# Value products with stationary values, normalised probabilities, and expert weights through other pools

## The chip, the cores and the metric

One core of a Trainium2 chip runs the whole kernel. The metric is the device time of one execution in microseconds; the number of a kernel is the median of its runs. The engines named here are PE (TensorE, with its weight loads as PEld), DVE (VectorE), ACT (ScalarE), POOL (GpSimd) and SP (SyncE, which issues the DMAs).

## The reference

256 tokens of width 1024 pass two blocks of two layers each, all in float32. Cut to what matters here:

```python
# first block, layer i
q, k, v = project_qkv(x, w_qkv[i], cos, sin)            # 16 query heads, 4 key/value heads, 64 wide
a = moba_attention(q, k, v) if i == 0 else sliding_window_attention(q, k, v, sinks)
x = layer_norm(alpha * x + a @ w_o[i], ...)
f = swiglu(x, ...) if i == 0 else moe_swiglu(x, ...)    # 8 experts, top 2, d_ff 3584
x = layer_norm(alpha * x + f, ...)
x = x + (p[i] @ w_ple_proj[i]) * sigmoid(x @ w_ple_gate[i])
# sliding window
probs = e / (jnp.sum(e, axis=-1, keepdims=True) + jnp.exp(sink - m))
out = einsum('bnkgqj,bnjkd->bnqkgd', probs, vv)
# second block, layer l: gated delta rule and a dilated causal attention (8 heads, 64 wide), side by side,
# then a gated FFN with a short convolution
```

All three attentions are a softmax over scores and a product with the values. The mixture of experts reads all eight experts' weights, 8 x 3 x 1024 x 3584 numbers.

## The kernel before

The program is one long list of operations. A planner (class `Plan`) takes them with their data dependencies, gives every tile a slot of a pool and writes out an order for each engine; SP's DMAs are in one such order too. All operations are issued in one helper, so they all carry line 756 in the profile (ACT's copies line 754, the loads of expert counts line 751). The pools in SBUF that matter: `raw` (5 slots, weights as they come), `hi` and `lo` (the split of a weight into two rounded parts, 6 and 5), `v4`, `w4`, `kv` (4, 8 and 2 slots), and `mx` (15 slots), which takes the place of `hi`, `lo` and `r4` while the experts run. PSUM has pools A, B and C with 2, 4 and 2 banks.

**Attention of the first block** (`first_layer`, `att_pair`, `att_out`, `part_T`; layers 0 and 1). The 256 queries are two blocks b of 128, the 16 heads two parts of eight, each part two groups of four. For a block and a part, `att_pair` makes the scores of both groups side by side in PSUM (C and B), the negative maximum on DVE and exp on ACT. `att_out` then takes one group at a time: it transposes the probabilities P (PE, copies out of PSUM), multiplies the transposed probabilities, stationary with 128 queries, by the values of a head with a column of ones behind them (65 columns, `va`), once per head and key block (nk = b + 1 blocks), takes the reciprocal of the 65th column and multiplies the 64 others by it. That gives heads along the columns; `part_T` transposes the result again, four transposes per block and part, and splits it for w_o. w_o comes in chunks of 256 rows, 128 partitions each (`load`).

**Dilated attention** (`att_pair("dilated", ...)` in the second block's layers). The same for eight heads, once per layer and block, with pool A.

**Experts** (`moe`). `route` gives each token a position in its experts, the counts are loaded into PE registers (line 751) and the largest count decides a branch (`overflow_experts`, lines 1634 and 294), which isn't taken here. `gather_pair` makes one-hot matrices on DVE and gathers the tokens of two experts with matmuls. Then each expert takes its three matrices in 84 chunks of 128 rows, 512 KB each: gate and up in three passes of 1024 and one of 512 columns, and down between them. Up to 64 tokens of an expert run as 64 stationary columns against 512 weight columns, two column tiles side by side; if it has more, a conditional part (line 733) adds 32-column tiles. Experts 1, 3, 6 and 7 (counted from 0) take that part here; the others don't. The chunks land in a ring of slots: `raw_moe` is a string of 28 of them, in which m, r, w, v and k stand for `mx`, `raw`, `w4`, `v4` and `kv`. A slot is fetched into when its last user is done, and SP takes its fetches in order, so that one that waits holds up all behind it. Ahead of the experts `fetch` asks for the first 22 chunks, in `raw`, `kv` and `mx`.

## Time and profile before

| | us |
|---|---|
| median of 3 runs | 2221.87 (2221.15 to 2225.56) |
| the profiled execution | 2224.77 |
| its span | 2223.0 |
| PE busy | 2102.1 (95%) |
| DVE busy | 984.3 (44%) |
| ACT busy | 751.7 (34%) |
| POOL busy | 224.7 (10%) |
| DMA, mean over the span | 251 GB/s |

The terms of a sum are taken from the profiled execution and set against its 2224.77 us. Where its stages lie: layer 0's attention to about 110 us, its FFN to 400, layer 1's attention to 477, router and branch to 510, the experts to 1420, then the second block with its dilated attentions around 1600 to 1652 and 1975 to 2030. A busy PE is not a PE at its peak, and the DMA share is that of the packets' time over 16 engines: at 1.03 and some 408 GB/s the queues are full.

### The profile page before, as it was taken

What the parts mean: (1) busy time and instruction counts of PE and PEld (TensorE: products, weight loads), DVE (VectorE), ACT (ScalarE), POOL (GpSimd) and SP (SyncE); (2) the same over time, 40 slices, a digit from 0 to 9 for tenths busy, and PEclk for the clock granted to TensorE, in tenths of its full rate; (3) what the DMA queues carried; (4) which work ended last, traced back from release to release, by engine and by line L of the source; (5) the groups of instructions that cost most, each with busy time, mean ns of one, the idle gap of its engine ahead of it and who ended that gap; (6) DMA issues with size and microseconds to landing.
All of it is one profiled execution on the core that took longest, in us unless ns stands there. A gap on an engine that the chain in (4) does not pass through costs nothing. (4 is left out here: it accounts for less than half of the span.)

```text
span 2223.0 us, 35510 instructions
## 1 busy us (share of the span) xinstructions
PE 2102.1 (95%) x14582; PEld 1449.2 (65%) x14582; DVE 984.3 (44%) x1670; ACT 751.7 (34%) x1141; POOL 224.7 (10%) x147
## 2 busy tenths in 40 slices
PE   8999999988799989998979999899999999999998
PEld 6899997763334323433233434479979997988997
DVE  6665467651010101010101001467687768768666
ACT  5544444420011101110110000356465556456554
POOL 0110001120000000000000000218020005411000
PEclk9999999989899999999999999999999999999999
DMA  7356664349999999999999998544455664435563
GB/s 251 111 165 192 184 184 152 114 159 345 404 388 370 373 404 409 385 372 404 408 404 394 369 396 326 188 145 144 130 170 183 190 183 141 124 97 187 175 194 117
DMA packets 246476, 557.48 MB, mean 251 GB/s; under 512 B 21320, under 2 KB 108552, under 8 KB 246280
## 3 DMA queue, kind: packets, MB, share of 16 engines
q1 hardware_dynamic: 246280, 554.72, 69.9%
q8 instruction: 141, 2.31, 0.4%
q14 instruction: 55, 0.45, 0.1%
HBM read 553.60 MB, written 1.05 MB: 250 GB/s over the span
## 5 line engine op out<-in xcount | busy, mean ns | idle before, releaser
L756 DVE TENSOR_TENSOR lo<-raw,hi 128x1024 fp32r<-128x1024 f32 x324 | 404.7, 1257 | 200.3 <-PE B L756 94.6
L756 ACT ACTIVATE hi<-raw 128x1024 fp32r<-128x1024 f32 x364 | 382.2, 1062 | 292.8 <-PE B L756 123.5
L756 PE MATMUL B<-r,hi 128*128 128x256 f32 x2112 | 388.2, 282 | 0.0
L756 PEld LDWEIGHTS B<-r,hi 128*128 128x128 f32 x2112 | 342.0, 191 | 17.7
L756 PE MATMUL B<-mx,w 128*64 128x512 f32 (+3 forms) x2188 | 327.9, 458 | 10.6 <-DMA mx<-in_w_exp_up_dram 8.4
L756 PE MATMUL A<-hi,r 128*128 128x512 f32 x896 | 334.3, 410 | 0.9 <-DVE v L756 0.6
L756 PE MATMUL B<-r,lo 128*128 128x256 f32 x1056 | 298.6, 283 | 0.0
L756 PEld LDWEIGHTS B<-mx,w 128*32 128x32 f32 (+1 forms) x2188 | 111.0, 124 | 153.1 <-issue 104.3
L756 PEld LDWEIGHTS B<-r,lo 128*128 128x128 f32 x1056 | 201.5, 191 | 0.0
L756 PEld LDWEIGHTS A<-hi,r 128*128 128x128 f32 x896 | 171.1, 191 | 32.2 <-DVE v L756 1.4
L756 PE MATMUL C<-hi,r 128*128 128x512 f32 x512 | 185.1, 400 | 1.1 <-ACT kv L756 1.1
L756 DVE MEMSET B<- 128x256 f32 (+1 forms) x64 | 15.7, 245 | 370.0 <-ACT w L756 366.6
L756 PE MATMUL A<-lo,r 128*128 128x512 f32 x448 | 177.4, 396 | 0.2 <-DVE lo L756 0.2
L756 PE MATMUL B<-w,w 128*128 128x128 f32 (+4 forms) x1252 | 168.4, 363 | 0.3 <-PEq L733 0.3
L756 PE MATMUL A<-mx,v 128*32 128x256 f32 (+1 forms) x960 | 162.1, 491 | 0.2 <-PEq L733 0.2
L754 ACT ACTIVATE v<-C 128x512 f32<-128x512 f32 (+2 forms) x63 | 29.4, 467 | 379.8 <-PE C L756 336.0
L756 DVE TENSOR_TENSOR w<-w,B 128x256 f32<-128x256 f32 (+2 forms) x79 | 41.8, 529 | 247.9 <-PE B L756 229.7
L756 POOL TENSOR_TENSOR lo<-raw,hi 128x1024 fp32r<-128x1024 f32 x40 | 102.0, 2563 | 487.8 <-ACT hi L756 367.4
L756 PEld LDWEIGHTS B<-w,w 128*128 128x128 f32 (+2 forms) x1252 | 104.5, 155 | 51.4 <-issue 39.6
L756 ACT ACTIVATE w<-B 128x256 f32<-128x256 f32 (+3 forms) x95 | 44.7, 475 | 264.8 <-PE B L756 242.9
L756 PEld LDWEIGHTS C<-hi,r 128*128 128x128 f32 x512 | 98.5, 192 | 18.8 <-ACT kv L756 1.9
L756 PE MATMUL B<-raw,w 128*64 128x512 f32 (+3 forms) x648 | 100.9, 463 | 1.3 <-DMA raw<-in_w_exp_up_dram 1.0
(239 smaller groups left out, 2602.1 us busy)
## 6 DMA issues: line engine op xcount, KB each, us to landing
mx<-in_w_exp_up_dram SPq DMA_DIRECT2D x124, 512.0 KB, 10.2
mx<-in_w_exp_down_dram SPq DMA_DIRECT2D x120, 512.0 KB, 10.3
mx<-in_w_exp_gate_dram SPq DMA_DIRECT2D x119, 512.0 KB, 8.0
raw<-in_ffn_up_dram SPq DMA_DIRECT2D x88, 512.0 KB, 3.7
raw<-in_w_in_dram SPq DMA_DIRECT2D x56, 512.0 KB, 3.8
raw<-in_w_exp_down_dram SPq DMA_DIRECT2D x48, 512.0 KB, 10.2
w<-in_w_exp_up_dram SPq DMA_DIRECT2D x46, 512.0 KB, 10.2
raw<-in_ffn_down_dram SPq DMA_DIRECT2D x44, 512.0 KB, 4.5
```

The costliest lines, as they stand in the source:

```text
L754: eng.activation(args[0], args[1], AF.Copy)
L756: getattr(eng, method)(*args, **kw)
```

## The change

- In all attentions the values are the stationary operand now, in 64 columns, without the column of ones. The transposed probabilities of a group stream past: four heads at once (512 columns) in the first block, where the four share a key/value head, one head (128 columns) in the dilated attention. The two groups write the two halves of one PSUM tile (`att_values`), heads along the partitions, so the second transposition is gone and `split_ps` reads the result.
- Since a row of the result no longer belongs to one query, the probabilities are normalised ahead: exp adds up its row (`accum_out`), DVE takes the reciprocal and multiplies P, 128x512 at a time. The sink's share is added before that.
- The rows of w_o come in the heads' new order: two transfers over 64 partitions for each chunk (`by_heads`).
- Expert weights: the ring is 24 slots of `mx`, `raw` and `w4`; `v4` and `kv` are no longer in it. Ahead of the experts 28 chunks are asked for, 7 of them (into `raw` and `kv`) before the switch of the region.
- The count loads have no bounds check, and the first one-hot matrices are made before the branch.

The diff, cut to that:

```diff
         if method == "values_load":
-            kw["to"].cell[0] = self.nc.values_load(args[0], engines=[mybir.EngineType.PE], min_val=0, max_val=S)
+            kw["to"].cell[0] = self.nc.values_load(args[0], engines=[mybir.EngineType.PE],
+                                                       skip_runtime_bounds_check_because="it is the sum of 256 zeros and ones")
...
-        self.raw_first = [("raw", RAW)] * RAW + [("kv", 2)] * 2 + [("mx", 15)] * 15
-        size = {"m": ("mx", 15), "r": ("raw", RAW), "w": ("w4", 8), "v": ("v4", 4), "k": ("kv", 2)}
-        self.raw_moe = [size[c] for c in "mrmwmrmvmwmkmrmwmrmvmwmkmrmm"]
+        self.raw_first = [("raw", RAW)] * RAW + [("kv", 2)] * 2 + [("mx", 15)] * 15 + [("w4", 8)] * 4 + [("v4", 4)] * 2
+        size = {"m": ("mx", 15), "r": ("raw", RAW), "w": ("w4", 8)}
+        self.raw_moe = [size[c] for c in "mrmwmmrmwmmrmwmmrmwmmrmm"]
         self.fetched = {}
-        self.ahead = []
+        self.ahead, self.by_heads = [], False
...
             r0 = k0 + 128 * m * h
-            nc.sync.dma_start(raw, lambda r0=r0: w[span(r0, 128 * m), span(c0, n)].rearrange("(t p) c -> p t c", p=128))
+            if self.by_heads:
+
+                for s in range(2):
+                    r0 = k0 + 256 * s + 64 * m * h
+                    nc.sync.dma_start(raw[64 * s:64 * s + 64], w[r0:r0 + 64 * m, c0:c0 + n].rearrange("(t p) c -> p t c", p=64))
+            else:
+                nc.sync.dma_start(raw, lambda r0=r0: w[span(r0, 128 * m), span(c0, n)].rearrange("(t p) c -> p t c", p=128))
             raws.append(raw)
...
-        va = self.nc.tile([128, 2, HK, 65], F32, "va", "kv", 2)
-        self.nc.gpsimd.memset(va, 1.0)
+        va = self.nc.tile([128, 2, HK, 64], F32, "va", "kv", 2)
         return qT, kT, va
...
+                hs = slice(i0, i0 + per)
+                for i in range(i0, i0 + per):
+                    nc.scalar.activation(P[:, i], ps[:, i - i0], AF.Exp, bias=nm[:, i:i + 1], accum_out=den[:, i])
+                if kind == "swa":
+                    es = self.sm([128, per, 1], "es")
+                    nc.vector.tensor_tensor(out=es[:, :, 0], in0=ns, in1=self.nsink[:, 4 * g + i0:4 * g + i0 + per], op=OP.subtract)
+                    nc.scalar.activation(es, es, AF.Exp)
+                    nc.vector.tensor_tensor(out=den[:, hs], in0=den[:, hs], in1=es, op=OP.add)
+                nc.vector.reciprocal(den[:, hs], den[:, hs])
+                part = P[:, hs].rearrange("p i k j -> p i (k j)")
+                nc.vector.tensor_tensor(out=part, in0=part, in1=den[:, hs].to_broadcast([128, per, nk * 128]), op=OP.mult)
+        self.att_values(kind, va, b, [(heads, P) for _, heads, P, _, _ in groups], [t[k] for t in aT.tiles])
...
-        po = (self.pb if grouped else self.pa)([128, 4, 65], "po")
-        for i in range(4):
-            for kb in range(nk):
-                nc.tensor.matmul(po[:, i, :], lhsT=PT[:, i, kb, :], rhs=va[:, kb, heads[i][3], :],
-                                 start=kb == 0, stop=kb == nk - 1)
...
-        nc.vector.tensor_tensor(out=o, in0=po[:, :, 0:64], in1=den.to_broadcast([128, 4, 64]), op=OP.mult)
...
+        pool = self.pb if grouped else self.pa
+        PT = [self.heads_last(P, nk, pool) for _, P in groups]
+        po = pool([128, 4, 128], "po")
+        with nc.group():
+            for i in range(1 if grouped else 4):
+                hs = slice(None) if grouped else i
+                for kb in range(nk):
+                    for s, (heads, _) in enumerate(groups):
+                        nc.tensor.matmul(po[64 * s:64 * s + 64, hs], lhsT=va[:, kb, heads[i][3], :], rhs=PT[s][:, hs, kb, :],
+                                         start=kb == 0, stop=kb == nk - 1)
+        self.split_ps(po, *[t[:, :, b * 128:b * 128 + 128] for t in dst])
...
-    def gather_pair(self, e, xs, pos):
-
-        nc = self.nc
+    def pair_one_hots(self, e, pos):
+
         P = self.r2([128, 2, 256], "P")
         for j in range(2):
             for b in range(2):
-                nc.vector.tensor_scalar(P[:, b, 128 * j:128 * j + 128], self.iota, pos[:, b, e + j:e + j + 1], None, op0=OP.is_equal)
+                self.nc.vector.tensor_scalar(P[:, b, 128 * j:128 * j + 128], self.iota, pos[:, b, e + j:e + j + 1], None, op0=OP.is_equal)
+        return P
+
...
         self.raw_tags = self.raw_first
-        for name, c0, n in (("gate", 0, 8), ("up", 0, 8), ("gate", 1024, 6)):
-            for k in range(n):
-                key = "w_exp_" + name, 0, 128 * k, c0
-                self.raws = len(self.fetched) - 1
-                self.fetched[key] = self.weights(*key[:3], 1, c0, 1024)
+        keys = [("w_exp_" + name, 0, 128 * k, c0) for c0 in (0, 1024) for name in ("gate", "up") for k in range(KT)]
+        for i in range(len(self.fetched), n):
+            key = keys[i]
+            self.raws = i - 1
+            self.fetched[key] = self.weights(*key[:3], 1, key[3], 1024)
+        self.raw_tags = [("raw", RAW)]
...
+        P = self.pair_one_hots(0, pos)
         self.overflow_experts(logits, rank, xs, pos)
         gg = self.gates(logits, rank, "gg")
         widths = [1024, 1024, 1024, 512]
         starts = [sum(widths[:c]) for c in range(len(widths))]
         n = len(widths)
         self.raw_tags, self.raws = self.raw_moe, 0
-        xg = self.gather_pair(0, xs, pos)
+        xg = self.gather_pair(P, xs)
...
         def heads(part):
             for b in range(2):
-                t = self.tb([128, 512], "a")
-                self.att_pair(kind, qT, kT, va, b, part, t)
-                self.part_T(t, b, aT, 4 * part)
+                self.att_pair(kind, qT, kT, va, b, part, aT, part)
 
...
             nc.vector.scalar_tensor_tensor(self.x[b][:, sl], self.x[b][:, sl], ALPHA, acc, op0=OP.mult, op1=OP.add)
 
+        self.by_heads = True
         self.dense_tok(aT, a["w_o"][i], 0, range(2), ev_a, 0, 4, pools=[self.pa])
...
             for b in range(2):
                 nc.gpsimd.tensor_scalar(self.x[b], self.x[b], ALPHA, None, op0=OP.mult)
         else:
+            self.fetch(RAW + 2)
...
         self.dense_tok(xT, w, 2056, range(3), ev, pools=[self.pa])
         for b in range(2):
-            t = self.tb([128, 512], "a")
-            self.att_pair("dilated", qT, kT, va, b, 0, t)
-            self.part_T(t, b, mT, 4)
```

PE in layer 1, the last block and part, from the transposes to the value products. B, A and C are PSUM tiles, `v_140` to `v_143` probabilities and their transposes, `v_153` and `v_154` the result, `kv_145` the values, `hi`/`lo` and `r` a weight and its operand. Before:

```order
L756 MATMUL B_137<-ident_91,v_141 128x128 x4
L756 MATMUL B_138<-ident_91,v_140 128x128 x4
L756 MATMUL A_147<-hi_1_74,r_1_64 128x512
L756 MATMUL A_147<-lo_1_82,r_1_64 128x512
L756 MATMUL A_147<-hi_1_74,r_1_70 128x512
L756 MATMUL B_137<-kv_145,v_143 128x65 x8
L756 MATMUL B_136<-ident_91,v_140 128x128 x4
L756 MATMUL B_138<-kv_145,v_142 128x65 x4
L756 MATMUL B_139<-ident_91,v_154 128x128
L756 MATMUL B_138<-kv_145,v_142 128x65 x4
```

and after:

```order
L757 MATMUL B_136<-ident_91,v_141 128x128 x4
L757 MATMUL B_138<-ident_91,v_143 128x128
L757 MATMUL A_147<-hi_1_75,r_1_64 128x512
L757 MATMUL A_147<-lo_1_80,r_1_64 128x512
L757 MATMUL A_147<-hi_1_75,r_1_70 128x512
L757 MATMUL B_137<-ident_91,v_143 128x128 x4
L757 LDWEIGHTS identb_92
L757 MATMUL C_158<-identb_92 128x512
L757 LDWEIGHTS identb_92
L757 MATMUL C_158<-identb_92 128x512
L757 LDWEIGHTS identb_92
L757 MATMUL C_158<-identb_92 128x512
L757 MATMUL B_136<-v_142,kv_145 64x512
L757 MATMUL B_136<-v_140,kv_145 64x512
L757 MATMUL B_136<-v_142,kv_145 64x512
L757 MATMUL B_136<-v_140,kv_145 64x512
```

The products by 65 columns and the transposes of `v_154` are gone; three matmuls that only occupy PE (`identb`) and four value products, two by two, stand there now.

SP, from w_o's last chunks to the first expert weights. Before:

```order
L756 DMA raw_150<-in_w_o_dram 128x2x512
L756 DMA raw_151<-in_w_o_dram 128x2x512
L756 DMA mx_2_3989<-in_w_exp_gate_dram 128x1024
L756 DMA mx_2_3986<-in_w_exp_up_dram 128x1024
L756 DMA mx_2_3987<-in_w_exp_up_dram 128x1024
L756 DMA raw_152<-in_w_exp_gate_dram 128x1024
```

and after:

```order
L757 DMA raw_150<-in_w_o_dram 64x2x512 x2
L757 DMA raw_151<-in_w_o_dram 64x2x512 x2
L757 DMA raw_148<-in_w_exp_gate_dram 128x1024
L757 DMA raw_152<-in_w_exp_gate_dram 128x1024
L757 DMA kv_144<-in_w_exp_gate_dram 128x1024
L757 DMA raw_149<-in_w_exp_gate_dram 128x1024
L757 DMA raw_150<-in_w_exp_gate_dram 128x1024
L757 DMA kv_145<-in_w_exp_gate_dram 128x1024
L757 DMA raw_151<-in_w_exp_gate_dram 128x1024
L757 DMA mx_2_3939<-in_w_exp_up_dram 128x1024
L757 DMA mx_2_3940<-in_w_exp_up_dram 128x1024
L757 DMA mx_2_3945<-in_w_exp_up_dram 128x1024
```

The first fetch into `mx`, which needs the region to be free, stood ahead of those into `raw` and `kv`; it stands behind seven of them now.

DVE at the end of the routing (`most` is the largest count, `r_169` takes the one-hots). Before:

```order
L756 SCALAR_TENSOR_TENSOR pos_187<-B_137,sm_121 128x16
L756 TENSOR_REDUCE sm_124<-B_136 128x1
L756 CAST count_189<-B_136 128x8
L756 CAST most_188<-sm_124 128x1
L1634 TENSOR_LOAD most_188
L294 COMPARE_AND_BRANCH
```

and after:

```order
L757 SCALAR_TENSOR_TENSOR pos_187<-B_138,sm_128 128x16
L757 CAST count_189<-B_139 128x8
L757 TENSOR_REDUCE sm_125<-B_139 128x1
L757 TENSOR_SCALAR r_169<-iota_106,pos_187 128x128
L757 CAST most_188<-sm_125 128x1
L757 TENSOR_SCALAR r_169<-iota_106,pos_187 128x128 x3
L1654 TENSOR_LOAD most_188
L294 COMPARE_AND_BRANCH
```

Four one-hots stand ahead of the branch now; they stood behind it, with the gather.

## Rows read from the trace of the kernel before

**Rows 1.** Windows by stage: busy us (count) of each engine, PEclk, DMA share, GB/s.

```profile
400.00:477.00 77.00, 73.80 (x479) 61.18 (x478) 49.58 (x116) 33.42 (x72) 8.51 (x4) 1.00 0.17 57
...
644.00:763.00 119.00, 118.51 (x1044) 50.66 (x1043) 13.75 (x35) 11.78 (x24) 1.04 (x2) 1.00 0.95 374
763.00:868.00 105.00, 93.27 (x527) 34.12 (x527) 12.34 (x30) 9.78 (x21) 1.04 (x2) 0.95 1.03 406
868.00:988.00 120.00, 119.51 (x1049) 50.95 (x1047) 13.75 (x35) 11.77 (x24) 1.04 (x2) 1.00 0.97 381
988.00:1092.00 104.00, 89.12 (x402) 30.40 (x400) 12.23 (x30) 9.78 (x22) 1.04 (x2) 0.93 1.03 406
1092.00:1207.00 115.00, 99.82 (x567) 38.56 (x566) 12.76 (x31) 11.56 (x24) 1.04 (x2) 0.94 1.01 399
...
1600.00:1652.00 52.00, 49.64 (x317) 42.01 (x316) 42.42 (x59) 34.71 (x59) 13.08 (x9) 0.97 0.57 184
```

**Rows 2.** Timeline of PE in layer 0: start us, us, engine, line, operation, count.

```profile
79.50 0.82 PE L756 MATMUL B<-ident,v 128*128 128x128 f32 x6
80.16 1.00 PE L756 MATMUL B<-kv,v 128*128 128x65 f32 x8
...
83.04 1.89 PE L756 MATMUL B<-kv,v 128*128 128x65 f32 x16
84.77 0.39 PE L756 MATMUL B<-ident,v 128*128 128x128 f32 x2
```

**Rows 3.** Timeline of PE: score records on row tiles, then two weight chunks.

```profile
72.28 0.27 PE L756 MATMUL C<-kv,v 64*128 64x128 f32 x1
...
72.39 0.27 PE L756 MATMUL C<-kv,v 64*128 64x128 f32 x1
...
1263.82 1.03 PE L756 MATMUL A<-mx,v 128*64 128x512 f32 x4
1264.68 1.03 PE L756 MATMUL A<-raw,v 128*64 128x512 f32 x4
```

**Rows 4.** Groups by form: weight loads, count, busy us, mean ns of one.

```profile
L756 PEld LDWEIGHTS B<-mx,w 128*64 128x64 f32 x1100 | 77.1, 138 | 132.7 <-issue 101.1 <-DMA mx<-in_w_exp_up_dram 14.1 <-DMA mx<-in_w_exp_gate_dram 4.9
```

**Rows 5.** Groups by form on DVE and ACT: mean ns behind the busy us.

```profile
L756 DVE TENSOR_TENSOR w<-w,w 128x512 f32<-128x512 f32 x30 | 24.5, 815 | 7.7 <-ACT w L756 5.2 <-DVE w L756 0.5
...
L756 DVE TENSOR_TENSOR v<-B,sm 128x256 f32<-128x256 f32 x16 | 6.8, 422 | 0.4
...
L756 ACT ACTIVATION_READ_ACCUMULATOR w<-x 128x1 f32 x16 | 3.0, 187 | 0.0
```

**Rows 6.** Windows of 10 us in layer 1, columns as in rows 1.

```profile
440.00:450.00 10.00, 10.00 (x84) 7.85 (x83) 6.99 (x17) 3.93 (x14) 1.72 (x1) 1.00 0.01 2
450.00:460.00 10.00, 9.08 (x72) 8.14 (x70) 9.04 (x24) 6.77 (x15) 2.39 (x1) 1.00 0.00 0
```

**Rows 7.** Timeline of SP's queue: three of its issues.

```profile
476.96 0.34 SPq L756 DMA_DIRECT2D mx<-in_w_exp_gate_dram  x1
...
511.16 0.35 SPq L756 DMA_DIRECT2D w<-in_w_exp_up_dram  x1
...
524.16 0.33 SPq L756 DMA_DIRECT2D raw<-in_w_exp_gate_dram  x1
```

**Rows 8.** Line 751 (count loads; ns min/median/max, first and last start), then DVE and PE.

```profile
L751 PEldq TENSOR_LOAD <-count x8: 297/303/497, 492.0 to 497.2; - x8
L751 PEldq FUSED_REGOPS  x8: 146/146/160, 492.6 to 497.6; - x8
L751 PEldq SEQ_ASSERT  x8: 18/18/24, 492.8 to 497.8; - x8
...
504.65 1.41 DVE L756 TENSOR_SCALAR r<-iota,pos 128x128 fp32r<-128x128 f32 x4 [12.57 <-PEq L294]
...
506.13 3.59 PE L756 MATMUL C<-r,xs 128*128 128x256 f32 x24 [3.19 <-DVE sm L756]
```

**Rows 9.** Waits of PE in 510 to 1420: us in total, times, longest.

```profile
PE B L756 <- DMA v<-in_w_exp_gate_dram: 34.9, 4, 11.1
```

More of the change, by code (lines that the diff above doesn't have):

```diff
@@ L1147, in att_pair @@
                     for kb in range(nk):
-                        for ps, (_, heads, _, _) in zip(pss, groups):
+                        for ps, (_, heads, *_) in zip(pss, groups):
                             pr, s, kp, _ = heads[i0 + i]
@@ L1153, in att_pair @@
                                              stop=i == per - 1 and kb == nk - 1)
-            for ps, (g, heads, P, nm) in zip(pss, groups):
+            for ps, (g, heads, P, nm, den) in zip(pss, groups):
                 ns = nm[:, i0:i0 + per]
@@ L1158, in att_pair, with heads_last @@
                     nc.vector.tensor_tensor(out=ns, in0=ns, in1=self.nsink[:, 4 * g + i0:4 * g + i0 + per], op=OP.min)
-                for i in range(per):
-                    nc.scalar.activation(P[:, i0 + i], ps[:, i], AF.Exp, bias=nm[:, i0 + i:i0 + i + 1])
-        for g, heads, P, nm in groups:
-            self.att_out(kind, va, b, g, heads, P, nm, a)
-    def att_out(self, kind, va, b, g, heads, P, nm, a):
+                hs = slice(i0, i0 + per)
[10 more added lines that the diff above has]
+        self.att_values(kind, va, b, [(heads, P) for _, heads, P, _, _ in groups], [t[k] for t in aT.tiles])
+    def heads_last(self, P, nk, pool):
         nc = self.nc
-        grouped = kind != "dilated"
-        nk = b + 1
         per = 4 // nk
@@ L1170, in att_out @@
         for i0 in range(0, 4, per):
-            ps = (self.pb if grouped else self.pa)([128, per, nk, 128], "PTp")
+            ps = pool([128, per, nk, 128], "PTp")
             for i in range(per):
@@ L1175, in att_out, with att_values @@
             self.copy_out(PT[:, i0:i0 + per], ps)
-        po = (self.pb if grouped else self.pa)([128, 4, 65], "po")
-        for i in range(4):
-            for kb in range(nk):
-                nc.tensor.matmul(po[:, i, :], lhsT=PT[:, i, kb, :], rhs=va[:, kb, heads[i][3], :],
-                                 start=kb == 0, stop=kb == nk - 1)
-        den = self.sm([128, 4, 1], "den")
-        if kind == "swa":
-            es = self.sm([128, 4], "es")
-            nc.vector.tensor_tensor(out=es, in0=nm, in1=self.nsink[:, 4 * g:4 * g + 4], op=OP.subtract)
-            nc.scalar.activation(es, es, AF.Exp)
-            nc.vector.tensor_tensor(out=den, in0=po[:, :, 64:65], in1=es[:, :, None], op=OP.add)
-            nc.vector.reciprocal(den, den)
-        else:
-            nc.vector.reciprocal(den, po[:, :, 64:65])
-        if grouped:
-            o = a[:, (g % 2) * 256:(g % 2) * 256 + 256].rearrange("p (h d) -> p h d", d=64)
-        else:
-            o = a.rearrange("p (i s d) -> p i s d", s=2, d=64)[:, :, g, :]
-        nc.vector.tensor_tensor(out=o, in0=po[:, :, 0:64], in1=den.to_broadcast([128, 4, 64]), op=OP.mult)
+        return PT
+    def att_values(self, kind, va, b, groups, dst):
+        nc = self.nc
+        nk = b + 1
+        grouped = kind != "dilated"
+        pool = self.pb if grouped else self.pa
[9 more added lines that the diff above has]
+        self.split_ps(po, *[t[:, :, b * 128:b * 128 + 128] for t in dst])
     def ple_proj(self, i):
@@ L1457, in weights, with fetch @@
         return raw
-    def fetch(self):
+    def fetch(self, n):
         self.raw_tags = self.raw_first
-        for name, c0, n in (("gate", 0, 8), ("up", 0, 8), ("gate", 1024, 6)):
-            for k in range(n):
-                key = "w_exp_" + name, 0, 128 * k, c0
-                self.raws = len(self.fetched) - 1
-                self.fetched[key] = self.weights(*key[:3], 1, c0, 1024)
+        keys = [("w_exp_" + name, 0, 128 * k, c0) for c0 in (0, 1024) for name in ("gate", "up") for k in range(KT)]
[4 more added lines that the diff above has]
+        self.raw_tags = [("raw", RAW)]
     def tiled(self, acc, slots, units, count, first, last):
@@ L1593, in moe @@
         nc, a, tc = self.nc, self.a, self.tc
-        self.fetch()
+        self.fetch(len(self.raw_first))
         rank, pos = self.route(logits)
@@ L1704, in ev_o @@
                 self.layer_norm(b, [held[b, 0], held[b, 1]], gm, bm, ready)
+        self.by_heads = True
         self.dense_tok(aT, a["w_o"][i], 0, range(2), ev_o, 4, 4)
+        self.by_heads = False
         if i == 0:
@@ L2034, in mixer @@
         for b in range(2):
-            t = self.tb([128, 512], "a")
-            self.att_pair("dilated", qT, kT, va, b, 0, t)
-            self.part_T(t, b, mT, 4)
+            self.att_pair("dilated", qT, kT, va, b, 0, mT, 1)
             out(b, mT)
```

13 lines of the change are left out of this document (8 added, 5 removed).

## Prediction

> **What bounds the kernel now.** I first read the table of stages [rows 1]. In the attention stretches PE is busy nearly all the time (73.8 of 77 us in 400 to 477, 49.6 of 52 in 1600 to 1652), so PE work taken out there counts, unless another engine then becomes late. DVE is at 49.6 of 77 us there. In the experts two kinds alternate. In 763 to 868 and 988 to 1092 the DMA share is 1.03 at 406 GB/s while PE is busy for 93 of 105 and 89 of 104 us: DMA-bound. A chunk of 512 KB takes 524288 B / 406 GB/s = 1.29 us there. In 644 to 763 and 868 to 988, where the tail group also runs, PE is full and the DMA share is 0.95 and 0.97: PE-bound. Against 1.03 the DMA stands still for 0.08/1.03 x 119 = 9.2 us and 0.06/1.03 x 120 = 7.0 us, and for 2.2 us in 1092 to 1207. These 18.4 us matter, since the experts behind them are DMA-bound and wait for bytes that were not fetched.
>
> Then the stretch before the experts [rows 6, 7]: from 440 the DMA moves almost nothing, and SP's first expert fetch goes out at 476.96. Last the front of the experts [rows 8]: eight count loads, the branch, four one-hots on DVE, and the gather at 506.13.
>
> **First layers' attention, PE.** Before, each of the two layers has 48 value matmuls (two records each) and 16 transposes of the output. Sixteen records take 84.77 - 83.04 = 1.73 us, so 0.216 us for a matmul; six transposes take 80.16 - 79.50 = 0.66 us, 0.11 each [rows 2]. That is 10.4 + 1.8 = 12.1 us a layer. After, there are 12 matmuls of 64 stationary columns by 512. The nearest rows are the experts' own: four such records, two column tiles side by side, start 0.86 us before the next four [rows 3]. Twelve matmuls are 24 records, 5.2 us. PE loses 6.9 us a layer.
>
> The rows show loads of 64 columns at 138 ns [rows 4] that leave the 0.86 us as it is: four of them would be 0.55 us. The Trainium skill, TensorE: Matmul & The Clock Gate (The mechanism), says that a weight load overlaps running matmuls only when the row group differs, which two tiles over all 128 rows do not; by that, 24 loads would add 3.3 us a layer and 48 loads 6.6 us in each dilated layer, 19.9 us in all, as much as the change takes out. The rows of the experts disagree, so I keep the loads at nothing and let the rule stand as a reason for the first rival.
>
> **What takes its place.** DVE gets 12 normalisations of 128x512 per layer. No row has that form; between 422 ns (half the columns) and 815 ns (two full operands) I take 0.75 us, 9.0 us [rows 5]. It loses 8 products of 0.42 us, 3.4 us: +5.6 us net. ACT gets 32 accumulator reads of 187 ns, 6.0 us, hidden by its idle half. DVE would stand at 55 of about 70 us, but it is not evenly spread: in 450 to 460 it is busy for 9.04 of 10 us already, with PE at 9.08 [rows 6]. There the normalisation stands between exp and transposes, in DVE's queue, with the next scores' reduction behind it, and PE waits for both. In layer 1's last pair nothing but three filler matmuls stands between the transposes and the value matmuls. So I count about half of the PE gain: layer 0 **-4 us** (-7 to +2), layer 1 **-3 us** (-7 to +3); the upper ends are 12 exposed steps of 0.75 us less the 6.9 us.
>
> w_o now comes as 32 transfers over 64 partitions in place of 16. SP issues each in about 0.34 us [rows 7]: 16 more are 5.4 us on a queue that is idle there, hidden by the w_o chunks that are on their way before the attention ends. The Trainium skill, DMA: Bandwidth & Descriptors (Rules for kernel authors), advises against splitting a transfer over partition halves, because both share the same engines; in this stretch the engines are four fifths idle, so by the rule too only those 5.4 us could show.
>
> **Dilated layers.** Before, 24 value matmuls of 0.216 us and 8 transposes of 0.11 us: 6.1 us. After, 24 matmuls of 64 x 128. The nearest row is a score pair on two row tiles, with 0.11 us from one pair of records to the next [rows 3]; 24 such pairs are 2.6 us, without overlap 5.3. So -3.4 us a layer at best and -0.8 at worst, against 6 normalisations (4.5 us on DVE, and on the chain of the last block). For the two layers together I take **-3 us** (-7 to +4).
>
> **Front of the experts.** A count load is 0.303 us and its check 0.146 and 0.018; the eight start 5.2/7 = 0.74 us apart [rows 8]. Without the check they stand 0.30 to 0.58 apart: -1.3 to -3.5 us. The four one-hots (1.41 us from 504.65) are made before the branch, so that the gather can start when PE's branch is done: about -1.5 us. Together **-4 us** (-5 to -1).
>
> **The early fetches.** SP's order lets 7 chunks go ahead of the region switch and 28 in place of 22 ahead of its branch. That looks like 7 x 1.29 = 9 us. I count it at **0**. Before, SP sends eight more from 511.16, 30 chunks in all, and the next one leaves at 524.16 [rows 7]: it waits for a buffer that PE frees some 15 chunks into the first expert. After, only two follow the 28, and chunk 30 waits for the same place. The DMA will be idle longer before it; from there on it hangs on PE's start.
>
> **The pools.** The ring shrinks from 28 buffers, v and k among them, to 24. How far SP can fetch ahead is set by the narrowest places, where a fetch waits for a chunk used shortly before. Counted in the order of both kernels, the room is 19.3 chunks on average and 6 or 7 at the narrowest before, 16.7 and 4 or 5 after. Before, experts 1 to 5 have five places with under ten chunks while a tail is behind, and these five cost the 18.4 us, 3.7 each. After, three such places stand in a tail expert or right behind one (experts 1, 3 and 4), and two of four chunks in the DMA-bound experts 2 and 4. Three by 3.7 is 11; the narrower room adds a chunk, 1.3, and the other two 0 to 4, since PE there waits for data and frees a buffer at once. That is 12 to 16 against 18.4: **-3 us**, with -8 if only one stop stays and +8 if seven places cost 3.7 each.
>
> The order in which chunks are needed comes closer to that in which they are fetched (at most 7 apart, 13 before). PE's four waits for v-buffered gate chunks are 34.9 us [rows 9]; in DMA-bound experts they only move, but the last one, ahead of the two PE-bound experts, counts: **-2 us** (-4 to 0).
>
> **Sum.** -4 - 3 - 3 - 4 + 0 - 3 - 2 = -19 us. The profiled execution took 2224.77 us, which becomes 2205.8; it lies 2.9 above the median of the three runs, 2221.87, so the forecast is **2203 us**.
>
> **Rivals.**
> 1. The attention gives nothing: weight loads that show, or DVE's normalisations, fill what PE loses. For it: DVE at 9.04 of 10 us. Against it: 450 to 460 is the worst stretch of the layer, and PE is the fuller engine in the others. Then -9 us, 2213.
> 2. The early fetches pay in full: chunk 30's buffer is free when SP asks for it. For it: the empty DMA from 440 on. Against it: SP already stands there now, between its eight issues from 511.16 and the next at 524.16. Then -28 us, 2194.
> 3. Slower: the smaller ring. If four buffers less mean that the fetches stop four chunks earlier once in every expert, each stop is 4 x 1.29 = 5.2 us; in experts 1 to 5 25.8 us in place of -3, so -16 + 25.8 = +10 us, 2232. It decides from 16/5.2, that is from the fourth expert on; in the two tail experts alone it gives -6 us, 2216. For it: room of four chunks in experts 2 and 4. Against it: in a DMA-bound expert the fetches run at PE's heels anyway.
> 4. The change does not do what it says, since PE waits at the new places and runs fillers: this is rival 1 at its worst, near the time before.
>
> **How the numbers follow.** Forecast 0.52 (2196 to 2212), rival 1 0.17, rival 2 0.09, rival 3 in two experts 0.10 and in four or more 0.07, no net change 0.05. The limit of what can be told from no change is 0.2%, 4.4 us, so faster means under 2217.4. That holds for the forecast, rival 2, most of rival 1 and half of the two-expert case: 0.80; within 0.2% 0.11; slower 0.09. The range leaves out about one in ten at each end: 2187 to 2219.
>
> **What would show it.** Right: the first layers' attention about 3 to 4 us shorter with PE still full and DVE over 80%; the gather right behind PE's branch, the DMA idle for some 15 us around 505 to 520; the experts' first matmul to the end of the last expert shorter by about 5 us. Wrong: PE idle behind DVE in the attentions (rival 1); chunk 30 leaving by 515 (rival 2); DMA shares under 1.0 in experts 2 and 4 (rival 3).

## The result, and the profile after

| | before | after |
|---|---|---|
| median of 4 runs, us | 2221.51 (2220.65 to 2225.56) | 2199.90 (2195.16 to 2201.29) |
| the profiled execution | 2224.77 | 2195.16 |
| its span | 2223.0 | 2193.4 |
| PE busy | 2102.1 | 2086.8 |
| DVE busy | 984.3 | 989.9 |
| ACT busy | 751.7 | 767.0 |

The ratio is 0.9895 [0.9883, 0.9906]: by the medians 21.6 us faster, against a forecast of 18.9 (2221.87 to 2203). The profiled executions differ by more, 29.6, since the one of before lies 3 us above its median and the one of after 5 us below.

The table of stages of the kernel after (columns as in [rows 1], which it answers, with one slice of 10 us in layer 1 as in [rows 6]):

```profile
400.00:465.00 65.00, 61.23 (x356) 43.99 (x355) 51.35 (x120) 35.24 (x104) 7.67 (x3) 1.00 0.40 106
440.00:450.00 10.00, 7.65 (x48) 4.79 (x44) 9.72 (x24) 6.33 (x24) 3.30 (x2) 1.00 0.32 106
621.00:742.00 121.00, 120.67 (x1058) 51.89 (x1056) 13.76 (x35) 11.90 (x24) 1.04 (x2) 1.00 0.95 379
742.00:850.00 108.00, 97.83 (x547) 32.66 (x545) 12.86 (x34) 10.76 (x23) 1.04 (x2) 1.00 1.00 402
850.00:967.00 117.00, 116.31 (x1035) 50.25 (x1031) 11.73 (x28) 12.39 (x26) 1.04 (x2) 1.00 0.98 389
967.00:1073.00 106.00, 92.79 (x419) 28.35 (x417) 12.76 (x34) 10.94 (x24) 1.04 (x2) 0.98 1.00 400
1073.00:1184.00 111.00, 96.79 (x551) 36.09 (x549) 10.93 (x24) 11.63 (x26) 1.04 (x2) 0.98 1.03 417
1580.00:1630.00 50.00, 45.14 (x307) 36.73 (x306) 40.98 (x57) 35.90 (x76) 20.37 (x12) 1.00 0.55 170
```

The first and the last row are the attention stretches. PE is full nearly all the time as before, DVE has risen to 51.35 of 65 us, and from 440 to 450 it is busy for 9.72 of 10 us while PE falls to 7.65. The five rows from 621 to 1184 are experts 1 to 5. Where the queues are full, the DMA moves 417 GB/s at the same share of 1.03 that went with 406 before. Nothing in the forecast speaks of that; much of what follows is about it.

For every kernel that was run, this is the profiled execution less that of before, cut at the same instructions: start to the first attention (42 us in before), layer 0's attention (to 122), its FFN (to 349), layer 1's attention and routing to the first count load (492), from there to the first gather (506), the experts (to 1420), and the second block to the end. The column on the right goes by the median of the runs of before that each kernel is set against (2221.0 to 2221.5).

| kernel | start | att 0 | FFN | att 1 | front | experts | block 2 | sum | median less before |
|---|---|---|---|---|---|---|---|---|---|
| forecast | 0 | -4 | 0 | -3 | -4 | -5 | -3 | -19 | -18.9 |
| after | -3.7 | -4.0 | 0.1 | -2.0 | -4.1 | -9.7 | -6.3 | -29.6 | -21.6 |
| a_shift | -3.4 | -4.0 | 0.1 | -1.1 | -3.8 | **2.8** | -9.3 | -18.8 | -14.2 |
| a_oldring | -4.2 | -4.0 | 0.1 | -2.1 | -4.1 | -10.2 | -6.8 | -31.2 | -25.9 |
| att | -4.1 | -4.0 | 0.1 | -1.0 | -0.4 | -5.2 | -3.2 | -17.8 | -20.0 |
| att_front | -3.3 | -4.0 | 0.1 | -1.5 | -4.0 | -7.6 | -6.5 | -26.6 | -17.0 |
| front_only | -2.4 | 0.0 | 0.0 | 0.0 | -3.9 | -0.1 | -2.7 | -9.0 | -3.3 |
| moe | -4.3 | 0.0 | 0.0 | 0.6 | -3.7 | **2.7** | -0.2 | -4.8 | -1.7 |
| ring | -3.7 | 3.6 | -0.1 | 0.4 | -0.2 | -5.8 | 4.5 | -1.2 | +4.1 |
| fetch | -2.2 | 3.5 | -0.1 | 0.4 | -0.2 | 1.6 | 3.5 | 6.3 | +5.9 |
| b_shift | -0.4 | 0.0 | 0.0 | -4.3 | 0.0 | **-8.4** | 0.4 | -12.6 | -9.0 |
| b_mxonly | -3.1 | 0.0 | 0.0 | 0.1 | 0.5 | **-7.2** | 1.0 | -8.7 | -4.5 |
| b_rawonly | -3.5 | -0.1 | 0.0 | 0.7 | 0.6 | -0.6 | -0.3 | -3.1 | 0.0 |
| b_halves | -2.3 | 3.4 | 0.2 | -1.1 | 0.0 | -0.1 | -0.2 | -0.2 | +3.1 |

The first column is not the change. The windows of the kernel before at its start (columns as above):

```profile
0.00:10.00 10.00, 5.38 (x21) 2.93 (x22) 4.40 (x31) 3.22 (x5) 1.50 (x10) 0.99 0.74 221
10.00:20.00 10.00, 9.78 (x37) 6.93 (x36) 8.55 (x19) 7.06 (x9) 0.00 (x0) 0.84 1.07 379
20.00:30.00 10.00, 7.39 (x29) 5.29 (x28) 5.64 (x15) 5.23 (x8) 0.00 (x0) 0.84 0.99 348
30.00:40.00 10.00, 10.00 (x37) 8.02 (x37) 3.45 (x8) 2.79 (x4) 0.00 (x0) 0.82 0.55 183
```

From 10 to 40 us the granted clock is 0.84, 0.84 and 0.82 of full speed, that is, about a third of each slice at 1.2 in place of 2.4 GHz, after a first slice in which PE was busy for 5.38 of 10 us. In the kernel after it stays at 1.00 in all of them. 0.16, 0.16 and 0.18 of 10 us are 5 us at most, and kernels that leave the start as it is (front_only, b_mxonly, b_rawonly) come out 2 to 4 us ahead there too. Slices like these come and go elsewhere. From 350 to 370 before has 0.90 and 0.76, some 3.4 us short of full speed, and b_shift has 1.00 twice, which is most of its -4.3 in the column att 1. At 110 us ring, fetch and b_halves have a slice at 0.83, 1.7 of their 3.4 to 3.6 us in the column att 0; the rest goes with another order of layer 0's operations, which the planner wrote for these three. In ring (timeline of PE, columns as in [rows 2], with PE's wait behind):

```profile
110.42 1.97 PE L756 MATMUL B<-ident,x 128*128 128x128 f32 x8 [3.36 <-DVE x L756]
```

where before has two halves of this, the second with a wait of 1.86:

```profile
111.53 0.63 PE L756 MATMUL B<-ident,x 128*128 128x128 f32 x4 [1.86 <-DVE x L756]
```

The second block is long and has the most of such slices. Added up they are some 11 us short of full speed in before, 9 in after and 5 in a_shift. So a stage is read from a trace to about 2 us, and the column block 2 to several, unless several kernels agree, and the medians decide the rest.

### The profile page after: what moved, and what is told of

It is laid out like the page before. It is cut to its first block, busy times and chain, and to the rows that moved or that the text cites. A ratio compares the mean times of both kernels' runs of the same rounds, so it can differ in the third digit from the quotient of the medians.

```text
span 2193.4 us, 35412 instructions
## 1 busy us (share of the span) xinstructions
PE 2086.8 (95%) x14407; PEld 1410.7 (64%) x14407; DVE 989.9 (45%) x1678; ACT 767.0 (35%) x1256; POOL 243.1 (11%) x152
## 5 line engine op out<-in xcount | busy, mean ns | idle before, releaser
L757 DVE TENSOR_TENSOR lo<-raw,hi 128x1024 fp32r<-128x1024 f32 x315 | 394.3, 1260 | 190.5 <-PE B L757 95.3
L757 PE MATMUL B<-mx,w 128*64 128x512 f32 (+3 forms) x2428 | 347.0, 455 | 12.8 <-DMA mx<-in_w_exp_gate_dram 5.2
L757 PEld LDWEIGHTS B<-mx,w 128*64 128x64 f32 (+1 forms) x2428 | 119.0, 124 | 185.1 <-issue 113.7
L757 PE MATMUL A<-mx,v 128*32 128x256 f32 (+1 forms) x1208 | 195.3, 492 | 8.7 <-DMA mx<-in_w_exp_down_dram 6.3
L757 POOL TENSOR_TENSOR lo<-raw,hi 128x1024 fp32r<-128x1024 f32 x49 | 127.2, 2609 | 644.2 <-ACT hi L757 578.8
L757 PE MATMUL B<-w,w 128*128 128x128 f32 (+4 forms) x1328 | 179.9, 368 | 1.3 <-PEq L733 1.3
L757 PE MATMUL B<-raw,w 128*64 128x512 f32 (+3 forms) x884 | 131.4, 453 | 14.3 <-DMA raw<-in_w_exp_gate_dram 7.0
L757 PEld LDWEIGHTS A<-mx,v 128*32 128x32 f32 (+1 forms) x1208 | 57.1, 123 | 101.1 <-issue 64.3
```

Of the source, the lines that this page charges most:

```text
L757: getattr(eng, method)(*args, **kw)
```

## The experiments

**One part alone.** Four kernels each take one part of the change, or leave one out. `att` is the attention only, with the old ring, fetches and front: of the diff, all hunks of the attention, such as

```diff
-        va = self.nc.tile([128, 2, HK, 65], F32, "va", "kv", 2)
-        self.nc.gpsimd.memset(va, 1.0)
+        va = self.nc.tile([128, 2, HK, 64], F32, "va", "kv", 2)
...
+                        nc.tensor.matmul(po[64 * s:64 * s + 64, hs], lhsT=va[:, kb, heads[i][3], :], rhs=PT[s][:, hs, kb, :],
+                                         start=kb == 0, stop=kb == nk - 1)
```

> The attention part alone (stationary values, normalised probabilities, w_o in halves); ring, fetches, count loads and one-hots as before. Theory A (the forecast's terms): PE work taken out shows by about half, -10 us, 2211, with layer 0's attention about 4 us, layer 1's about 3 us and both dilated layers together about 3 us shorter. Theory B (all of it shows, and waits of the dilated layers go with it): -15 us or more, 2206. Rival (weight loads or DVE's normalisations fill what PE loses): within 4 us of 2221.5.

Measured 2201.07, ratio 0.9906 [0.9890, 0.9923], the case of theory B, 15 us or more; so 20 of the 21.6 us come with the attention. But in the trace 5.2 arise in the experts, where `att` changes no instruction. `moe` is everything but the attention; against the kernel after, the same hunks the other way round:

```diff
-        va = self.nc.tile([128, 2, HK, 64], F32, "va", "kv", 2)
+        va = self.nc.tile([128, 2, HK, 65], F32, "va", "kv", 2)
+        self.nc.gpsimd.memset(va, 1.0)
```

> All of the change but the attention part: ring of 24, 28 early fetches, count loads without the check, early one-hots. The forecast's terms: -4 (front), 0 (fetches), -3 (ring) and -2 (order), 2212. If the first expert gains 9 us beyond the front, as the trace of the changed kernel has it, whatever the reason: about -14 us, 2208, with the first expert ending some 13 us earlier. If this needs the attention part's other placing of slots: under -9.

Measured 2219.41, ratio 0.9997 [0.9987, 1.0008]: the last of the three cases, a gain under 9 us. Its gather comes 3.7 us earlier by the front, and its experts take 2.7 us longer. `ring` changes one line and `fetch` the early fetches, with the order in which they are asked for:

```diff
-        self.raw_moe = [size[c] for c in "mrmwmrmvmwmkmrmwmrmvmwmkmrmm"]
+        self.raw_moe = [size[c] for c in "mrmwmmrmwmmrmwmmrmwmmrmm"]
...
-        self.raw_first = [("raw", RAW)] * RAW + [("kv", 2)] * 2 + [("mx", 15)] * 15
+        self.raw_first = [("raw", RAW)] * RAW + [("kv", 2)] * 2 + [("mx", 15)] * 15 + [("w4", 8)] * 4 + [("v4", 4)] * 2
...
+        keys = [("w_exp_" + name, 0, 128 * k, c0) for c0 in (0, 1024) for name in ("gate", "up") for k in range(KT)]
...
+            self.fetch(RAW + 2)
```

> Only the string of the ring is changed, 24 slots of mx, raw and w4 in place of 28 with v4 and kv; 22 early fetches as before. Theory O (the order in which chunks are needed against the order in which they come was what cost the first expert 16 us of PE waits): the waits on gate chunks in v4 go, the first expert ends 7 to 9 us earlier, and the whole is -5 to -9 us, 2213 to 2216. Theory F (the early fetches did it): the first expert ends as before, and the smaller ring costs up to 8 us, 2221 to 2229.

> Only the fetches ahead of the experts are changed: 28 in place of 22, seven of them before the switch of the region; ring as before. Forecast: 0, since chunk 30 waits for PE in both, 2219 to 2223. Theory F: the first expert ends about 9 us earlier and the whole gains up to that, 2212 to 2216. Theory O: the waits on v4 chunks stay, so nothing is gained.

Measured 2225.25, 1.0022 [1.0008, 1.0035], and 2226.99, 1.0025 [1.0012, 1.0037]. Both are slower, `fetch` beyond every range expected. Expert 0 does end earlier, as theory O had it for `ring` (9.3 us) and theory F for `fetch` (11.8 us); by the end of the experts `ring` keeps 5.8 of that, and `fetch` has lost it and 1.6 more. The rest of the loss of both stands elsewhere, in layer 0 (3.6 and 3.5 us, above) and behind the experts. The second block, in which neither changes an operation, from the end of the last expert to the end of the second dilated attention (windows, columns as above), before:

```profile
1419.60:2036.35 616.75, 593.12 (x3998) 527.31 (x3998) 451.15 (x719) 344.77 (x515) 160.92 (x92) 0.98 0.50 152
```

and with the small ring:

```profile
1413.85:2035.10 621.25, 595.81 (x4005) 527.71 (x4005) 455.40 (x717) 344.17 (x512) 163.02 (x96) 0.99 0.48 151
```

621.25 against 616.75 us, and POOL has 96 operations where it had 92: the planner, which places both blocks in one list, wrote the second block in another order (`fetch`: 96 too). In `moe`, which holds both edits, it is the old order (92 operations, 616.6 us). So the times of `ring` and `fetch` alone do not price the ring; their experts do.

**Where the weights lie.** The records of the packets gave the lead. Of the 4096 B packets from 520 to 1160 us, 38% take exactly 159 ns in before, and a quarter more than 165; in after 98% take 159. Every kernel is of one kind or the other: mixed packets in before, moe, ring, fetch, front_only (38 to 44% at 159), flat ones in after, att, att_front, a_oldring (95 to 98%). What the second kind shares is the attention's `va` without its column of ones, 4096 in place of 4160 B. It is a `kv` slot, there are two, and all that lies behind them in SBUF moves down by 128 B. So two kernels move tiles and nothing else: `b_shift` is the kernel before with `kv` slots 64 B longer, `a_shift` the kernel after with the old length.

```diff
-            n = -(-info["bytes"] // 4)
+            n = -(-info["bytes"] // 4) + 16 * (tag == "kv")
```

> The kernel before, order for order, with 128 bytes more per partition in the two slots of kv together, so that every tile behind them lies elsewhere: mx at 0 modulo 512 in place of 384, raw and w4 at 480 in place of 352. Theory P (the place of the weight tiles in SBUF sets how long a 4 KB packet takes: 159 ns in the kernels with the attention part, 162 to 164 in those without, and the attention part made the kv slots 4096 bytes in place of 4160): the packets fall to 159 ns, a chunk from 1.28 to 1.25 us, and the whole is 5 to 14 us faster. Rival Q (something else in the attention part, such as the w_o transfers, does it): no change, 2221.

> The changed kernel, order for order, with kv slots of 4160 bytes as before the change, so that mx, raw and w4 lie where they lay before it. Theory P: packets of 162 to 164 ns, 1.28 us a chunk, and 5 to 14 us slower than 2199.9. Rival Q: 2200.

Measured: `b_shift` 2212.42, 0.9959 [0.9945, 0.9972], 96% of the packets at 159 ns; `a_shift` 2207.28, 0.9937 [0.9916, 0.9959], 43%. The same instructions, 9.0 us faster than before and 7.4 us slower than after, as theory P had it. Two more kernels ask which tile it is. `b_mxonly` pads a small tile ahead of the experts' region (`fw`), so that only the region, with the `mx` slots, moves by 128 B; `b_rawonly` pads both, so that `raw` and `w4` move by 128 and the region by 256 (first and second line below).

```diff
+            n = -(-info["bytes"] // 4) + 32 * (tag == "fw")
...
+            n = -(-info["bytes"] // 4) + 16 * (tag == "kv") + 32 * (tag == "fw")
```

> The kernel before, instruction for instruction, with 128 B put behind a small tile, so that only the tiles of the experts' region (the fifteen mx tiles among them) lie 128 B later, while raw, w4, v4 and kv stay. If the place of the mx tiles, which take 15 chunks of each 28, sets the time of a packet: 159 to 160 ns and 2212 to 2214 us. If it is the place of raw and w4: 161 to 164 ns and 2220 to 2223 us.

> The kernel before, instruction for instruction, with raw, w4 and what follows them 128 B later and the experts' region 256 B later, so that mx stands as before modulo 256 B while raw and w4 don't. If the place of mx modulo 256 B sets the time of a packet: 161 to 164 ns and 2220 to 2223 us. If that of raw and w4 does: 159 to 160 ns and 2212 to 2214 us. In between, some 2217 us, if each tile's packets go by its own place.

Measured: `b_mxonly` 2216.46, 0.9977 [0.9968, 0.9987], 98% at 159 ns; `b_rawonly` 2220.99, 1.0003 [0.9989, 1.0017], 36%. The packets of both are those of the first case, that the place of `mx` decides. But the time of `b_mxonly` is 2.5 us above its range: in the experts it gains nearly what `b_shift` does (7.2 and 8.4 us), by the medians half of it (4.5 and 9.0), and why is open. The same window of 20 us in full flow (columns as above), before:

```profile
1130.00:1150.00 20.00, 18.46 (x122) 9.62 (x120) 1.40 (x4) 3.22 (x7) 0.52 (x1) 1.00 1.04 397
```

`b_rawonly`:

```profile
1130.00:1150.00 20.00, 18.37 (x124) 9.72 (x124) 1.57 (x5) 3.22 (x7) 0.52 (x1) 1.00 1.04 398
```

`b_mxonly`:

```profile
1130.00:1150.00 20.00, 14.90 (x104) 8.19 (x102) 1.57 (x5) 2.54 (x6) 0.52 (x1) 1.00 1.04 414
```

and after:

```profile
1130.00:1150.00 20.00, 14.01 (x63) 4.90 (x61) 0.98 (x3) 0.99 (x3) 0.52 (x1) 0.91 1.03 419
```

The last two numbers are the DMA share and GB/s: 1.04 and 397 or 398 in the first two, 1.04 and 414, 1.03 and 419 in the others. The queues are as full, and 4 to 5% more bytes pass. This window is the far end; from 770 to 860 us, in the first DMA-bound expert, it is 406 GB/s in before and in `b_rawonly`, and in `b_mxonly`:

```profile
770.00:860.00 90.00, 80.58 (x479) 29.99 (x477) 7.16 (x17) 5.41 (x13) 1.04 (x2) 0.96 1.03 414
```

2% more. The granted clock does not go with it: over the experts it is 0.97 in before, `b_rawonly` and `b_shift`, 0.98 in `b_mxonly`, and 0.99 in after as in `a_shift`. In all 14 traces the packets' time goes by the start of the `mx` slots: a multiple of 256 B where the packets are flat (166144, 166400), 128 B past one where they are mixed (166272, 166528). `raw` starts 96 B past a multiple of 256 in before and in `b_mxonly` and 224 past in after and in `b_rawonly`, a kernel of either kind each, so its place doesn't decide.

Writing into `mx` is enough; PE need not read from it. From 495 to 503 us only chunks for `mx` are still on their way in before (first line below, of SP), and PE first reads one at 513.51 (second line):

```profile
490.95 7.52 SPq L756 DMA_DIRECT2D mx<-in_w_exp_gate_dram  x6
...
513.51 1.08 PE L756 MATMUL B<-mx,w 128*64 128x512 f32 x4
```

In these 8 us 66% of the packets take 159 ns in before and 62% in `b_rawonly`, against 98% in `b_mxonly` and in `b_shift`.

The Trainium skill, DMA: Bandwidth & Descriptors (How a descriptor splits into AXI transactions), says that a transfer is cut at multiples of 256 B, so that one that starts elsewhere takes one piece more and fetches bytes that nobody needs. It speaks of what is read; here the written side was moved. By that account 4096 B from 128 B past a boundary take 132 beats of 32 B in place of 128, 3% more; an estimate, and `mx` agrees in sign and about in size (over the 4096 B packets under 200 ns, 520 to 1160 us, the mean is 162.5 ns in before and 159.1 in `b_mxonly`, 2% more). But `raw`, `w4` and `v4` start off such a boundary in every kernel here, and where `mx` is on one, nearly all packets take 159 ns, theirs among them. So the rule is not shown for them. Why `mx` alone decides stays open, as does a kernel with every weight tile on a boundary, which wasn't run.

**The front.** `front_only` has the count loads without the check and the one-hots ahead of the branch.

```diff
+            kw["to"].cell[0] = self.nc.values_load(args[0], engines=[mybir.EngineType.PE],
+                                                       skip_runtime_bounds_check_because="it is the sum of 256 zeros and ones")
...
+        P = self.pair_one_hots(0, pos)
         self.overflow_experts(logits, rank, xs, pos)
...
+        xg = self.gather_pair(P, xs)
```

> The kernel before with the front of the experts alone changed: the eight counts are loaded without a check of their range, and the one-hots of the first pair are made ahead of the counts. The forecast's term was -4 us at the gather of pair 0. Theory A, that an expert's end follows the transfers of weights once expert 2 is reached: the gather 4 us earlier and the kernel within 1.5 us of before, 2220 to 2222. Theory B, that the 4 us are kept to the end: 2217 to 2218. Packets as before, some 162 ns, since no weight tile moves.

Measured 2217.69, 0.9988 [0.9978, 0.9997]. The gather comes 3.9 us earlier, and the experts behind it are 0.1 us shorter: the gain is kept, and theory A falls.

**Halves.** `b_halves` is the kernel before with the w_o chunks in two transfers over 64 partitions each, in the old order of rows.

```diff
+            if self.halves:
+                for s in range(2):
+                    nc.sync.dma_start(raw[64 * s:64 * s + 64], w[r0:r0 + 128 * m, c0:c0 + n].rearrange("(t p) c -> p t c", p=128)[64 * s:64 * s + 64])
```

> The kernel before with w_o fetched in two transfers over 64 partitions each, rows in their old order. Theory P: packets as before (162 to 164 ns), and the split costs nothing or up to 5.4 us (16 issues more at 0.34 us): 2221 to 2227. Rival Q with w_o as the cause: 159 ns packets and 5 us or more faster.

Measured 2224.51, 1.0018 [1.0003, 1.0033]. Its packets are mixed as in before, so the halves are not what makes them flat. Its trace has 3.4 us more in layer 0's stage, where half of the new transfers stand; 1.7 of that is the slice at 0.83, and the order of operations differs there too. In layer 1, where the other half stands, it has 1.1 us less. So up to 3 us is what the halves can cost, and they are not told apart from the order.

**Put together.** `att_front` is attention and front without the pools and the order of need; `a_oldring` is the kernel after with the old ring of 28. The first is the edits of `att` and `front_only` in one; the second, against after:

```diff
-        self.raw_moe = [size[c] for c in "mrmwmmrmwmmrmwmmrmwmmrmm"]
+        size = {"m": ("mx", 15), "r": ("raw", RAW), "w": ("w4", 8), "v": ("v4", 4), "k": ("kv", 2)}
+        self.raw_moe = [size[c] for c in "mrmwmrmvmwmkmrmwmrmvmwmkmrmm"]
```

> The changed attention and the changed front together, with the old ring of 28 chunks and the old early fetch of 22, that is without the pools and the order of need. If the ring and the longer early fetch bring nothing or cost (theory A): 2195 to 2199, as fast as the changed kernel or faster, packets of 159 ns. If they bring the 3 to 5 us of the forecast's sum (theory B): 2203 to 2206.

> The changed kernel with the ring of 28 slots of before (v4 and kv in it); 28 early fetches, front and attention part as changed. The forecast's terms (ring -3, order -2): 5 us slower than the changed kernel, 2205, with PE waits on v4 gate chunks back. If the ring costs what the run with the ring alone shows (+4): 2196.

Measured: `att_front` 2203.93, 0.9933 [0.9915, 0.9951]; `a_oldring` 2195.58, 0.9886 [0.9858, 0.9913]. `att_front` is 3 us above `att`, though it has one gain more; with four runs each, over 8.7 and 7.4 us, the two are not told apart. `a_oldring` is 5 to 8 us below both, and its interval lies just under that of `att_front`, so early fetches and order of need do seem to pay beside the new places. `a_oldring` is the fastest kernel here, 4.3 us below after by the medians; the intervals overlap, and in the experts the two traces agree to 0.5 us.

## Why the forecast came out, step by step

The time was right, and the sum behind it was not: one term was missing, and another had the wrong sign. That these two about cancel, and the time lands 3 us from 2203, is luck. Without the missing term it would be the 2207.3 us of `a_shift`, which the range of 2196 to 2212 holds too.

**Layer 0, -4: right.** -4.0 in all five kernels that have the new attention. PE there (timeline, columns as in [rows 2]):

```profile
74.69 1.08 PE L757 MATMUL B<-v,kv 128*64 128x512 f32 x4
75.70 0.66 PE L757 MATMUL B<-ident,v 128*128 128x128 f32 x4
...
78.83 1.52 PE L757 MATMUL B<-ident,v 128*128 128x128 f32 x11 [0.21 <-DVE r L757]
80.19 0.59 PE L757 MATMUL C<-identb 128*128 128x512 bf16 x2
80.98 1.99 PE L757 MATMUL B<-v,kv 128*64 128x512 f32 x8 [0.20 <-DVE v L757]
82.90 0.50 PE L757 MATMUL A<-hi,r 128*128 128x512 f32 x1
```

Four records are two matmuls, one for each group (74.69); eight are the four of a block with two key blocks (80.98). The next work starts 1.01 us after the four and 1.92 after the eight, so 0.96 to 1.01 for four where 0.86 was taken from [rows 3]; at 0.96, 24 records are 5.8 us a layer, not 5.2. The weight loads, by groups and forms (count, busy us, mean ns):

```profile
L757 PEld LDWEIGHTS B<-v,kv 128*64 128x64 f32 x48 | 3.2, 135 | 5.5 <-issue 3.4 <-DVE v L757 1.1 <-DVE r L757 0.4
```

Four of them at 135 ns are 0.54 us. If they did not overlap, four records would stand 1.4 us apart. In the dilated layers the records are shorter (PE timeline):

```profile
1612.97 1.97 PE L757 MATMUL A<-v,kv 128*64 128x128 f32 x32
1614.87 0.50 PE L757 MATMUL C<-hi,r 128*128 128x512 f32 x1
```

32 records in 1.90 us, 0.119 for a pair: 24 pairs are 2.85 us where 2.6 was taken and 5.3 was the bound without overlap. So two column tiles over the same rows load while others run, here as in [rows 3]. The rule of TensorE: Matmul & The Clock Gate (The mechanism) in the Trainium skill, by which the loads would add 3.3 us a layer and 6.6 in each dilated one, is not borne out. That half of PE's gain would be lost also held, and the rows show how: PE is kept busy by fillers (`identb`, 80.19) and waits 0.21 and 0.20 us for DVE (78.83, 80.98). Over the stage PE's busy time falls from 78.1 to 74.8 us, 3.3 of the 6.9.

**Layer 1, -3: right in sign, half in size.** -2.0, and -1.0 to -2.1 in the others. In `att`, `a_shift` and `att_front` the clock from 350 to 370 costs as much as in before (one slice at 0.66), and they have -1.0 to -1.5; after and `a_oldring` have 0.83 there. The normalisation costs more than was taken for it (groups and forms, DVE):

```profile
L757 DVE TENSOR_TENSOR v<-v,sm 128x512 f32<-128x512 f32 x36 | 30.6, 859 | 0.5
```

859 ns in place of 750, 12 of them 10.3 us a layer. With that DVE is full from 440 to 450, as the forecast feared for 450 to 460, and this is the price.

**Dilated layers, -3: right in sign.** -6.3 in after, -3.2 to -9.3 in the five kernels with the change, -2.7 to +1.0 in those that have the old order and the old attention. The column holds the whole second block with its slices of lower clock, of which `a_shift`, with the -9.3, loses least; a size is not to be had from it.

**Front, -4: right.** -4.1, and -3.7 to -4.1 in the others. Count loads, then PE around the branch:

```profile
L751 PEldq TENSOR_LOAD <-count x8: 297/307/491, 482.4 to 485.5; - x8
```

```profile
485.81 4.54 PE L757 MATMUL A<-identb 128*128 128x512 bf16 x13 [3.79 <-issue]
492.48 1.83 PE L757 MATMUL C<-r,xs 128*128 128x256 f32 x7 [2.13 <-PEq L294]
```

Eight loads from 482.4 to 485.5, 0.44 us apart where [rows 8] had 0.74, without the two checking instructions; PE starts the gather 2.13 us after its fillers, at the branch's end (`L294`), and DVE's one-hots no longer stand ahead of it.

**Early fetches, 0: right at chunk 30.** SP in the kernel after (columns as in [rows 7]):

```profile
430.90 0.82 SPq L757 DMA_DIRECT2D raw<-in_w_exp_gate_dram  x2
...
455.09 0.33 SPq L757 DMA_DIRECT2D kv<-in_w_exp_gate_dram  x1
...
466.22 1.28 SPq L757 DMA_DIRECT2D mx<-in_w_exp_up_dram  x3
...
483.81 1.64 SPq L757 DMA_DIRECT2D w<-in_w_exp_gate_dram  x2
...
497.54 0.33 SPq L757 DMA_DIRECT2D w<-in_w_exp_down_dram  x1
511.51 0.33 SPq L757 DMA_DIRECT2D raw<-in_w_exp_up_dram  x1
```

The first fetch leaves at 430.90, 46 us earlier than in [rows 7], and the first into `mx` at 466.22, 11 us earlier. SP stands all the same: after the 30th chunk (497.54) it waits until 511.51, where it waited until 524.16. That is 12.65 us earlier, and the gather, on which it hangs, is 13.65 us earlier. Rival 2 wanted it to leave at once; that it left before 515, the sign of rival 2, is only that the gather had moved. The sum had no gain in expert 0, though, and there `fetch` has 11.8 us, given back by the end of the experts.

**Pools and order, -5: this is the step that failed.** With `mx` at its old place the experts are 2.8 us longer, not 5 shorter (`a_shift`; 2.7 in `moe`). What happens can be followed at the ends of the experts (the last matmul with the down matrix). In after, expert 0 ends 22.8 us earlier than before, 9.1 more than the gather. PE's longest waits in expert 0, before:

```profile
PE B L756 <- DMA v<-in_w_exp_gate_dram: 11.1, 1, 11.1
PE B L756 <- DMA mx<-in_w_exp_up_dram: 4.9, 1, 4.9
```

and after:

```profile
PE A L757 <- DMA raw<-in_w_exp_down_dram: 3.4, 2, 3.2
PE B L757 <- DMA mx<-in_w_exp_gate_dram: 2.7, 3, 2.2
PE A L757 <- DMA mx<-in_w_exp_down_dram: 1.0, 1, 1.0
```

16 us of waits have become 7. The 11.1 is among the 34.9 us of [rows 9], of which the prediction let only the last wait count, since in DMA-bound experts they only move. But expert 1 is PE-bound and keeps most of the gain, 20.9 us at its end. Then it goes: in `a_shift` the lead is 20.1 us after expert 0, 17.8 after expert 1, 9.6 after expert 2 and 9.5 after expert 7. That is where the room was counted as narrow. But the narrow ring is not it alone, since `ring` gains 5.8 us in the experts, nor does it cost what rival 3 said: the larger ring of `a_oldring` is 0.5 us better. Counting stops at 3.7 us each was too coarse to give the sign, and its lower bound does not add up: one stop left would be 3.7 against 18.4, -14.7 and not -8. Why the two edits together give back what either gains by the end of expert 0 (9.3 and 11.8 us) is not settled.

**What the sum didn't have: the place of `mx`.** -7.2 and -8.4 in the experts of `b_mxonly` and `b_shift`, 4.5 to 9 us by the medians, and 7.4 less of it in `a_shift`. Without it the mechanisms of the forecast give what `a_shift` has, 14 us and not 19. The change in the diff that does it is `65` to `64` in the shape of `va`, which was read for its work on POOL and PE and not for where it puts the other tiles. By single traces, the pools and the order beside the new place would be worth 1.3 to 2.5 us in the experts (9.7 less 7.2, 8.4 or the 7.6 of `att_front`). But the place alone comes out between 5.2 (`att`) and 12.5 us (after against `a_shift`) there, so this is not shown.

**Rivals.** Rival 1 is out by layer 0 (-4.0 in five kernels), rival 2 by chunk 30, rival 3 by the experts of `ring` and `a_oldring`. Rival 4, near the time before, is out with rival 1.

## What to carry to other kernels

When a change resizes a tile, ask which tiles lie behind it and list their start addresses before and after: a kernel that pads one tile, with every instruction the same, prices that with one more kernel. Cut two traces at the same instructions and difference the stages before believing a total; a gain in a stage whose instructions did not change is the sign of a cause that the sum doesn't have. And where a planner orders the whole program, a part tried alone may come with another order far from it, so read its own stage and not its time.

## What the runs showed of the hardware

- The time of a 4096 B packet into SBUF depends on where the tiles lie: 159 ns nearly flat with `mx` on a multiple of 256 B, 159 to 172 ns with it 128 B past one; at the same DMA share of 1.03, 414 against 406 GB/s from 770 to 860 us.
- Two matmuls of 64 stationary columns over all 128 rows, side by side, hide most of each other's weight loads: 0.96 us for four records of 512 columns with 0.54 us of loads.
- A multiplication of 128x512 by a broadcast factor takes 859 ns on DVE, more than the same shape with two full operands (688 for `x<-x,w`, 815 for `w<-w,w`).
- The granted clock falls to 0.82 to 0.84 in slices of 10 us in some traces and stays at 1.00 in others whose instructions there are the same (from 10 to 40 us here). With it goes much of the spread between runs: the fastest of 25 runs of before (2216.92 us) had a mean granted clock of 0.982, the slowest (2227.05) one of 0.973.
